# How attention's softmax normaliser is turned into its reciprocal: Ln and Exp by ScalarE in place of a round trip through memory with VectorE's reciprocal

## The chip, the cores and the metric

The kernel runs on one core of a Trainium2 chip, in one launch. Its time is what one execution takes on the device, in microseconds (us). Five engines work side by side, each in its own program order: PE (TensorE, matmuls; PEld is its weight load), DVE (VectorE), ACT (ScalarE), POOL (GpSimd) and SP (SyncE, which here only issues DMAs). POOL and ACT issue DMAs too, in the order of their own instructions.

## The reference

A trunk of two layers on x of 1024 positions by 1024 channels, in fp32. Layer 0 mixes by a gated short convolution, layer 1 by dilated attention; a SwiGLU feed-forward follows each, and a norm ends it. What matters here is the attention (16 heads of 64):

```python
BRANCHES = ((128, 1), (512, 4), (2048, 16))       # window, dilation
...
bias = rel_bias[t5_bucket(jnp.clip(rel, 0) * dilation)]
s = s + bias...; s = jnp.where(mask, s, NEG_INF)
lse = jax.nn.logsumexp(s, axis=-1)
p = jnp.exp(s - lse[..., None])
o = einsum(p, v)                                  # one o and lse for each branch
...
alpha = jax.nn.softmax(jnp.stack(lses, axis=0), axis=0)
o = jnp.sum(alpha[..., None] * jnp.stack(outs, axis=0), axis=0)
return o.reshape(bsz, seq, D_MODEL) @ w_out
```

Weighting the branches by a softmax of their log-denominators is the same as one softmax over the keys of all three: the sum of exp(s) times v over the sum z of exp(s). So a query and head need one 1/z.

## The kernel before, in words

**Layout.** Activations lie with 128 channels on the partitions and 1024 positions along a row; such a [128, 1024] fp32 tile is a page, and 41 pages are handed out in rotation. The 8 banks of PSUM (`bank()`, 128x512 fp32) rotate too: a matmul into a bank waits until the engine that reads the bank's earlier content is done with it. An fp32 product is three matmuls over a high and a low part of each operand; `split` makes them, the high part by ACT (L142) and the low part by DVE (L143). The instructions are issued in the order of the code (`tc.manual_schedule()`), so what is written between two steps of one engine stands between them on the chip.

**Order of the program.** Layer 0 and its feed-forward come first; within it, from 942 us, `bias_tables` makes the tables of the relative bias, with an Exp (L529) and a Ln (L530) on a tile of 16x64. The attention follows, up to about 1470 us, then its feed-forward.

**The attention's loop.** `slot(n, ...)` runs for n = 0 to 16. Slot n computes the scores of head n and the product with the values (P·V) of head n−1, and between these it draws on a list of dense work: value tiles (L1512 to L1517), projections of q and k (L370 to L372, taken out by `emit`, L1138 to L1147) and the output product (L370 to L372, added to x by L492).

- `scores`: PE multiplies into banks (L1569, L1570); DVE reads each bank, adding the bias (L1580, L1589, L1606, L1611), and keeps a running maximum m (L1594 to L1620); POOL spreads the maximum over all partitions into mb (L1623, `partition_all_reduce`).
- `softmax`, in the second half of the slot: five times, DVE subtracts mb (L1631), and ACT takes the Exp in place (L1632).
- `values`, in slot n+1: PE multiplies the exponentials with v into two banks (L1642). v carries 64 columns of ones, so that half of each bank's partitions hold z, 64 times over. ACT copies z (L1665) and o (L1666) out.
- `finish(p)`, once both heads of a pair of heads p are done: 1/z. Its code is a generator whose steps are drawn at fixed places of the slots (the calls on `ending` and `extra`). POOL issues all its DMAs: two of the equal rows of z go to memory (zdram, L1674); come back as zc, 128 partitions by 16 (L1677); DVE takes the reciprocal (L1679); POOL writes it to memory (rdram, L1680) and reads it back spread over 64 partitions, twice, into z (L1683). Up to slot 14 the first four steps fall in an odd slot (two in the first half, one each later) and the end in the next even slot's first half.
- `attended()`: DVE multiplies o by z (L1730), POOL writes the pair to odram (L1731).
- The last pair is written apart: its first half takes DVE's reciprocals straight on the wide tile (L1704, twice 128x256), its second half goes through memory (L1691 to L1721).

`LAG` is 13: up to slot 13 the P·V runs in the slot's second half, after that in its first. From slot 12 on, written pairs are loaded again (tile oin), split, and multiplied by w_out.

Of the kernel before, what the change touches and what calls it, by code (L numbers as in the profile page):

```python
# [13 lines left out]
ALU = mybir.AluOpType  # L14
# [17 lines left out]
WARM = 10  # L32

# [65 lines left out]
def trunk(ctx: ExitStack, tc: tile.TileContext, x, gains_in, cwi, ck, cwo, wqkv, wo, relb,  # L99
# [397 lines left out]
    def bias_tables():  # L497
# [30 lines left out]
        nc.vector.tensor_tensor(out=d, in0=d, in1=m, op=ALU.subtract)  # L528
        nc.scalar.activation(d, d, AF.Exp)  # L529
# [940 lines left out]
    zdram = [[dram.tile([2, S], F32, name=f"{x}dram{n}") for x in "zr"] for n in range(NPAIR)]  # L1470

# [3 lines left out]
    def attention(norm, qk):  # L1475
# [159 lines left out]
        def values(p, a, st):  # L1635
# [27 lines left out]
            for ih in range(2):  # L1663
                s = slice(ih * HALF, (ih + 1) * HALF)
                nc.scalar.activation(z[n0, s], acc[ih][z0], AF.Copy)  # L1665
                nc.scalar.activation(o[n0, s], acc[ih][n0], AF.Copy)  # L1666
            yield

        def finish(p):

            o, z = OZ.pop(p)
            if p < NPAIR - 1:
                zd, rd = zdram[p]
                nc.gpsimd.dma_start(zd, z[0:65:64])  # L1674
                yield
                zc = scope["pool"].tile([128, 16], F32, name="zc", tag="zc", bufs=2)
                nc.gpsimd.dma_start(zc, bass.AP(zd.tensor, zd.offset, [[16, 128], [1, 16]]))  # L1677
                yield
                nc.vector.reciprocal(zc, zc)  # L1679
                nc.gpsimd.dma_start(bass.AP(rd.tensor, rd.offset, [[16, 128], [1, 16]]), zc)  # L1680
                yield
                for a in range(2):
                    nc.gpsimd.dma_start(z[64 * a:64 * a + 64], bass.AP(rd.tensor, rd.offset + a * S, [[0, 64], [1, S]]))  # L1683
                yield
                put_off.append((p, o, z))
                return

            zd, rd = zdram[p]
            wide = lambda t: bass.AP(t.tensor, t.offset, [[HALF, 2], [1, HALF]])
            thin = lambda t: bass.AP(t.tensor, t.offset, [[8, 128], [1, 8]])  # L1690
            nc.gpsimd.dma_start(wide(zd), z[0:65:64, HALF:])  # L1691
            zc = scope["pool"].tile([128, 8], F32, name="zl", tag="zl", bufs=1)
            nc.gpsimd.dma_start(zc, thin(zd))
            acts[p] = page("o_hi", F32R), page("o_lo", F32R)

            def scaled(c0, c1):
                q = slice(c0, c1)
                nc.vector.tensor_tensor(out=o[:, q], in0=o[:, q], in1=z[:, q], op=ALU.mult)
# [4 lines left out]
            for c in (0, 256):  # L1703
                nc.vector.reciprocal(z[:, c:c + 256], z[:, c:c + 256])  # L1704
                scaled(c, c + 256)
                if c:
                    parts(0)
                    nc.scalar.activation(scratch, eps, AF.Sqrt)
                yield

            def rest():
                scaled(HALF, S)
                parts(1)

            last_part.append(rest)
            yield
            ensure(ahead_ao + KT - AO_WIDE)
            nc.vector.reciprocal(zc, zc)
            nc.gpsimd.dma_start(thin(rd), zc)
            for a in range(2):  # L1720
                nc.gpsimd.dma_start(z[64 * a:64 * a + 64, HALF:],  # L1721
                                    bass.AP(rd.tensor, rd.offset + a * HALF, [[0, 64], [1, HALF]]))
# [13 lines left out]
        def slot(n, dense, ndense, late=0, hook=iter(())):  # L1736
# [30 lines left out]
            if lagged:  # L1767
                for i in range(8):
# [4 lines left out]
                    if a and ending and i in (0, 3):  # L1773
                        next(ending[-1])
                    if a == 0 and ending and i == 2:
                        run(ending.pop())
                run(sc)
            else:
# [3 lines left out]
                for i in range(8):  # L1782
# [6 lines left out]
                    if ending and i == 2:  # L1789
                        run(ending.pop())  # L1790
# [7 lines left out]
            for i in range(8):  # L1798
# [4 lines left out]
                if lagged and a and ending and i == 6:  # L1803
                    next(ending[-1])
# [35 lines left out]
        X[:] = [None] * KT  # L1840
        bias = {0: load_bias(0)}
# [236 lines left out]
```

## Time and profile before

| What | Value |
|---|---|
| Time, median of 3 runs | 2137.89 us (2135.56 to 2138.65) |
| Time of the profiled execution | 2136.81 us |
| Its span in the profile | 2135.0 us |
| Mean granted clock of TensorE | 0.996 |
| Stretches at half clock | 3.41 us from 1304.79, 6.83 us from 1355.99, the end from 2127.40 |
| z evictions, L1665, 64x512 | 32, 592 ns each |
| zc reciprocals, L1679, 128x16 | 7, 246 ns each |
| o*z, L1730, 128x1024 | 7, 1217 ns each |
| Waits of POOL, 1110 to 1440 us | zc on zdram 27.1 us in 6; rdram on zc 21.4 us in 5; z on rdram 16.7 us in 4 |

The time of an execution is a little more than its span, which runs from the first to the last instruction that the profiler shows. A row of a timeline gives start and duration in us, engine, line, operation, out<-in, and in brackets the idle time of the engine before it with the event that ended it. A row of waits gives the engine and line that waited, what for, the total, the number and the longest. L and a number is a line of the kernel before.

### The profile page before, as it was taken

The page shows a single profiled execution, that of the slowest core. Times are in us where ns is not written, and L with a number is a line of the kernel's source. Part 1 is how long each engine was busy: PE and PEld are TensorE (multiplying, and loading weights), DVE is VectorE, ACT ScalarE, POOL GpSimd, SP SyncE. Part 2 cuts the span into 40 slices and gives each one's busy share as a digit, 9 for nine tenths or more (in the row PEclk, how much of TensorE's full clock was granted, in tenths as well). Part 3 has the DMA queues.
Part 4 walks back from the last instruction along what each step waited for, and adds up shares of the span by engine and source line. Part 5 has one row for each costly group of instructions (what it writes and reads, how often), then busy time and mean ns, then how long its engine had stood idle before and what let it go on. Part 6 is the DMA issues. An engine that isn't in the chain of part 4 may idle for free. (4 is left out here: it accounts for less than half of the span.)

```text
span 2135.0 us, 31015 instructions
## 1 busy us (share of the span) xinstructions
PE 2103.4 (99%) x11082; PEld 1805.6 (85%) x11082; DVE 1744.7 (82%) x3273; ACT 1009.2 (47%) x1853; POOL 256.5 (12%) x375
## 2 busy tenths in 40 slices
PE   9999999999999999999999999999999999999998
PEld 7788888888888888877899998888788888888887
DVE  8898769988888888868967687777998888888876
ACT  7333426443444554446545544545543434456435
POOL 1000000110101000010322333221011101001000
PEclk9999999999999999999999999999999999999999
DMA  7322642333332576340767777765123333368432
GB/s 219 94 94 70 227 137 71 104 104 104 114 109 99 170 218 197 112 167 30 265 204 182 186 194 216 214 198 160 59 94 105 103 109 113 101 199 240 157 94 79
DMA packets 143449, 304.90 MB, mean 143 GB/s; under 512 B 48972, under 2 KB 55422, under 8 KB 143296
## 3 DMA queue, kind: packets, MB, share of 16 engines
q1 hardware_dynamic: 107488, 201.94, 31.5%
q0 software_dynamic: 28176, 86.29, 12.7%
q10 hardware_dynamic: 7632, 14.70, 1.8%
q8 instruction: 88, 1.44, 0.3%
q14 instruction: 65, 0.53, 0.1%
HBM read 212.48 MB, written 83.05 MB: 138 GB/s over the span
## 5 line engine op out<-in xcount | busy, mean ns | idle before, releaser
L572 PE MATMUL bank<-b,w 128*128 128x512 f32 x1952 | 760.9, 390 | 4.9 <-DVE w L143 4.7
L570 PE MATMUL bank<-b,w 128*128 128x512 f32 x1952 | 762.8, 391 | 2.5 <-ACT w L142 1.7
L571 PE MATMUL bank<-b,w 128*128 128x512 f32 x1952 | 760.4, 390 | 0.6 <-DVE b L881 0.6
L572 PEld LDWEIGHTS bank<-b,w 128*128 128x128 f32 x1952 | 366.4, 188 | 85.8 <-DVE w L143 9.6
L570 PEld LDWEIGHTS bank<-b,w 128*128 128x128 f32 x1952 | 366.7, 188 | 79.5 <-ACT w L142 2.8
L571 PEld LDWEIGHTS bank<-b,w 128*128 128x128 f32 x1952 | 366.7, 188 | 76.0 <-DVE b L881 1.2
L142 ACT ACTIVATE w<-combo 128x512 fp32r<-128x512 f32 (+2 forms) x488 | 249.1, 540 | 231.5 <-DVE combo L190 214.6
L143 DVE TENSOR_TENSOR w<-combo,w 128x512 fp32r<-128x512 f32 (+2 forms) x488 | 276.2, 579 | 37.8 <-ACT w L142 37.1
L576 ACT ACTIVATE part<-bank 128x512 f32<-128x512 f32 x186 | 110.8, 596 | 388.8 <-PE bank L572 385.3
L143 DVE TENSOR_TENSOR w<-raw,w 128x512 fp32r<-128x512 f32 (+2 forms) x342 | 189.6, 575 | 38.6 <-ACT w L142 38.6
L580 DVE TENSOR_TENSOR part<-part,bank 128x256 f32<-128x256 f32 (+1 forms) x366 | 170.5, 495 | 31.2 <-PE bank L572 16.7
L142 ACT ACTIVATE w<-raw 128x512 fp32r<-128x512 f32 (+2 forms) x342 | 166.7, 530 | 44.9 <-PE bank L572 12.2
L370 PE MATMUL bank<-w_hi,w 128*128 128x512 f32 (+1 forms) x400 | 153.3, 383 | 5.1 <-ACT w_hi L142 3.7
L371 PE MATMUL bank<-w_lo,w 128*128 128x512 f32 (+1 forms) x400 | 149.7, 374 | 1.2 <-DVE w_lo L143 1.2
L372 PE MATMUL bank<-w_hi,w 128*128 128x512 f32 (+1 forms) x400 | 149.7, 374 | 0.7 <-DVE w L143 0.7
L800 DVE TENSOR_TENSOR x<-x,bank 128x512 f32<-128x512 f32 x136 | 92.6, 681 | 29.2 <-PE bank L572 29.0
L492 DVE TENSOR_TENSOR x<-x,bank 128x512 f32<-128x512 f32 (+1 forms) x104 | 66.1, 641 | 56.6 <-PE bank L372 56.1
L190 DVE TENSOR_TENSOR combo<-raw 128x512 f32<-128x512 f32 (+1 forms) x172 | 111.1, 646 | 0.0
L370 PEld LDWEIGHTS bank<-w_hi,w 128*128 128x128 f32 x400 | 75.8, 189 | 18.5 <-ACT w_hi L142 3.9
L371 PEld LDWEIGHTS bank<-w_lo,w 128*128 128x128 f32 x400 | 75.7, 189 | 14.9 <-DVE w_lo L143 2.0
L372 PEld LDWEIGHTS bank<-w_hi,w 128*128 128x128 f32 x400 | 75.6, 189 | 14.8 <-DVE w L143 1.6
L563 DVE TENSOR_TENSOR b<-hin,b 128x512 fp32r<-128x512 f32 x126 | 79.5, 684 | 9.4 <-ACT b L562 9.4
(252 smaller groups left out, 3488.6 us busy)
## 6 DMA issues: line engine op xcount, KB each, us to landing
hin<-part SPq DMA_DIRECT2D x126, 256.0 KB
raw<-in_ffn_w_gate SPq DMA_DIRECT2D x44, 512.0 KB
raw<-in_ffn_w_up SPq DMA_DIRECT2D x44, 512.0 KB
part<-sum POOLq DMA_DIRECT2D x72, 256.0 KB, 2.3
raw<-in_ffn_w_down SPq DMA_DIRECT2D x48, 384.0 KB
raw<-in_attn_w_qkv SPq DMA_DIRECT2D x27, 512.0 KB
raw<-in_conv_w_in SPq DMA_DIRECT2D x24, 512.0 KB
part<-part POOLq DMA_DIRECT2D x36, 256.0 KB, 2.4
```

What stands on the lines that cost most here:

```text
L142: nc.scalar.activation(hi, src, AF.Copy)
L143: eng.tensor_tensor(out=lo, in0=src, in1=hi, op=ALU.subtract)
L190: eng.tensor_tensor(out=c, in0=a, in1=b, op=op)
L370: nc.tensor.matmul(b, whi[:, a], ahi[:, s], start=first, stop=False)
L371: nc.tensor.matmul(b, whi[:, a], alo[:, s], start=False, stop=False)
L372: nc.tensor.matmul(b, wlo[:, a], ahi[:, s], start=False, stop=last)
L570: nc.tensor.matmul(b, hi[:, a], bhi, start=start and k == 0, stop=False, skip_group_check=True)
L571: nc.tensor.matmul(b, hi[:, a], blo, start=False, stop=False, skip_group_check=True)
L572: nc.tensor.matmul(b, lo[:, a], bhi, start=False, stop=k == n - 1, skip_group_check=True)
L576: nc.scalar.activation(t, b, AF.Copy)
L580: nc.vector.tensor_tensor(out=t, in0=t, in1=b, op=ALU.add)
L800: nc.vector.tensor_tensor(out=X[n][:, half(h)], in0=X[n][:, half(h)], in1=b, op=ALU.add)
```

## The change

z leaves its banks through Ln in place of Copy, and `finish` is one Exp with scale −1 on the tile of 128x1024, so that z becomes exp(−ln z) = 1/z. The two buffers in memory, zc and the DMAs are gone. `finish` then has a single step, which runs in the first half of the odd slot (and in slot 14), and its pair is ready for `attended()` at the end of that same slot, where it had been the next even slot's. For the last pair, ACT does Exp on one half, DVE multiplies it and it is split, then the other half. Two calls name the activation table set that holds both Exp and Ln, one before the bias tables' Exp, one at the start of the attention.

```diff
@@ -30,6 +30,7 @@
 WINOGRAD = (1, 2, 6, 5, 7, 3, 4)
 DEEP, DEEPER = (2, 4), 10
 WARM = 10
+LN_EXP = "natural_log_exp_and_others"
 
 
 def paired(pairs, chunk, tiles):
@@ -526,6 +527,7 @@
         nc.vector.tensor_tensor(out=m, in0=b2, in1=b3, op=ALU.max)
         nc.vector.tensor_tensor(out=d, in0=b2, in1=b3, op=ALU.min)
         nc.vector.tensor_tensor(out=d, in0=d, in1=m, op=ALU.subtract)
+        nc.scalar.preload_act_table_set(LN_EXP)
         nc.scalar.activation(d, d, AF.Exp)
         nc.scalar.activation(d, d, AF.Ln, bias=1.0)
         nc.vector.tensor_tensor(out=b2, in0=m, in1=d, op=ALU.add)
@@ -1467,8 +1469,6 @@
 
     vdram = [dram.tile([S, 256], F32, name=f"vdram{g}") for g in range(NPAIR // 2)]
 
-    zdram = [[dram.tile([2, S], F32, name=f"{x}dram{n}") for x in "zr"] for n in range(NPAIR)]
-
     def blk(j):
         return (j // 4) * HALF + (j % 4) * 8
 
@@ -1662,7 +1662,7 @@
             z0 = slice(64 - 64 * a, 128 - 64 * a)
             for ih in range(2):
                 s = slice(ih * HALF, (ih + 1) * HALF)
-                nc.scalar.activation(z[n0, s], acc[ih][z0], AF.Copy)
+                nc.scalar.activation(z[n0, s], acc[ih][z0], AF.Ln)
                 nc.scalar.activation(o[n0, s], acc[ih][n0], AF.Copy)
             yield
 
@@ -1670,56 +1670,33 @@
 
             o, z = OZ.pop(p)
             if p < NPAIR - 1:
-                zd, rd = zdram[p]
-                nc.gpsimd.dma_start(zd, z[0:65:64])
-                yield
-                zc = scope["pool"].tile([128, 16], F32, name="zc", tag="zc", bufs=2)
-                nc.gpsimd.dma_start(zc, bass.AP(zd.tensor, zd.offset, [[16, 128], [1, 16]]))
-                yield
-                nc.vector.reciprocal(zc, zc)
-                nc.gpsimd.dma_start(bass.AP(rd.tensor, rd.offset, [[16, 128], [1, 16]]), zc)
-                yield
-                for a in range(2):
-                    nc.gpsimd.dma_start(z[64 * a:64 * a + 64], bass.AP(rd.tensor, rd.offset + a * S, [[0, 64], [1, S]]))
-                yield
+                nc.scalar.activation(z, z, AF.Exp, scale=-1.0)
                 put_off.append((p, o, z))
                 return
-
-            zd, rd = zdram[p]
-            wide = lambda t: bass.AP(t.tensor, t.offset, [[HALF, 2], [1, HALF]])
-            thin = lambda t: bass.AP(t.tensor, t.offset, [[8, 128], [1, 8]])
-            nc.gpsimd.dma_start(wide(zd), z[0:65:64, HALF:])
-            zc = scope["pool"].tile([128, 8], F32, name="zl", tag="zl", bufs=1)
-            nc.gpsimd.dma_start(zc, thin(zd))
+                yield
+
             acts[p] = page("o_hi", F32R), page("o_lo", F32R)
 
-            def scaled(c0, c1):
-                q = slice(c0, c1)
-                nc.vector.tensor_tensor(out=o[:, q], in0=o[:, q], in1=z[:, q], op=ALU.mult)
+            def scaled(h):
+                nc.vector.tensor_tensor(out=o[:, half(h)], in0=o[:, half(h)], in1=z[:, half(h)], op=ALU.mult)
 
             def parts(h):
                 split(o[:, half(h)], [t[:, half(h)] for t in acts[p]])
 
-            for c in (0, 256):
-                nc.vector.reciprocal(z[:, c:c + 256], z[:, c:c + 256])
-                scaled(c, c + 256)
-                if c:
-                    parts(0)
-                    nc.scalar.activation(scratch, eps, AF.Sqrt)
-                yield
-
             def rest():
-                scaled(HALF, S)
                 parts(1)
 
+            nc.scalar.activation(z[:, half(0)], z[:, half(0)], AF.Exp, scale=-1.0)
+            scaled(0)
+            parts(0)
+            yield
+            nc.scalar.activation(z[:, half(1)], z[:, half(1)], AF.Exp, scale=-1.0)
+            scaled(1)
+            nc.scalar.activation(scratch, eps, AF.Sqrt)
+            yield
             last_part.append(rest)
             yield
             ensure(ahead_ao + KT - AO_WIDE)
-            nc.vector.reciprocal(zc, zc)
-            nc.gpsimd.dma_start(thin(rd), zc)
-            for a in range(2):
-                nc.gpsimd.dma_start(z[64 * a:64 * a + 64, HALF:],
-                                    bass.AP(rd.tensor, rd.offset + a * HALF, [[0, 64], [1, HALF]]))
             ensure(ahead_ao + KT - AO_WIDE + 4)
             yield
 
@@ -1770,9 +1747,7 @@
                     if n or i % 2:
                         other(1)
                         used += 1
-                    if a and ending and i in (0, 3):
-                        next(ending[-1])
-                    if a == 0 and ending and i == 2:
+                    if a and ending and i == 0:
                         run(ending.pop())
                 run(sc)
             else:
@@ -1786,8 +1761,6 @@
                     if i >= late and i % 2 == 0:
                         other(1)
                         used += 1
-                    if ending and i == 2:
-                        run(ending.pop())
                 run(sc)
                 run(pv)
                 if a == 0:
@@ -1800,8 +1773,6 @@
                 next(pv, None)
                 if i == (2 if n > LAG + 1 else 5):
                     attended()
-                if lagged and a and ending and i == 6:
-                    next(ending[-1])
                 if not lagged and (i < FIN0 or i > SOFT):
                     next(extra, None)
                 if i in (1, 2):
@@ -1838,6 +1809,7 @@
                     add_to_x(n, {c: b})
 
         X[:] = [None] * KT
+        nc.scalar.preload_act_table_set(LN_EXP)
         bias = {0: load_bias(0)}
         load_kq(0)
         run(value_tiles(0, 0))
```

On ACT, in the bias tables (the tile d of 16x64, between a weight tile's splits), the order before:

```order
L529 ACT_TABLE_LOAD
L529 ACTIVATE d<-d 16x64
L530 ACT_TABLE_LOAD
L530 ACTIVATE d<-d 16x64
L142 ACTIVATE w<-raw 128x512
L880 ACTIVATE b<-x,gains 128x512
```

and now, where the split of `w` is L143:

```order
L530 ACT_TABLE_LOAD
L531 ACTIVATE d<-d 16x64
L532 ACTIVATE d<-d 16x64
L143 ACTIVATE w<-raw 128x512
L882 ACTIVATE b<-x,gains 128x512
```

The Ln has no table load of its own any more, and the split behind it moves up by one instruction.

On POOL, from slot 8 into slot 10 (kq is the projected q and k on its way to memory, odram a finished pair, mb the maximum of a slot), before:

```order
L1731 DMA odram_87<-o 128x1024
L1144 DMA kq_1_2951<-kq_hi 128x512
L1147 DMA kq_1_2951<-kq_lo 128x512
L1674 DMA zdram_103<-z 2x1024
L1677 DMA zc<-zdram_103 128x16
L1623 ISA mb<-m 128x1024
L1144 DMA kq_0_2950<-kq_hi 128x512
L1147 DMA kq_0_2950<-kq_lo 128x512
L1680 DMA rdram_104<-zc 128x16
L1144 DMA kq_0_2950<-kq_hi 128x512
L1147 DMA kq_0_2950<-kq_lo 128x512
L1683 DMA z<-rdram_104 64x1024 x2
```

and now:

```order
L1146 DMA kq_1_2935<-kq_hi 128x512
L1149 DMA kq_1_2935<-kq_lo 128x512
L1623 ISA mb<-m 128x1024
L1146 DMA kq_0_2934<-kq_hi 128x512
L1149 DMA kq_0_2934<-kq_lo 128x512
L1708 DMA odram_88<-o 128x1024
L1146 DMA kq_0_2934<-kq_hi 128x512
L1149 DMA kq_0_2934<-kq_lo 128x512
L1623 ISA mb<-m 128x1024 x2
```

The DMAs of z, zc and rdram are gone from between the others; mb of slot 9 stands behind the kq DMAs alone, and the write of a pair stands in the odd slot.

On DVE, where slot 14's subtractions end and slot 15 begins (lf is the next head's bias add, x the residual that takes the output product), before:

```order
L1631 TENSOR_TENSOR lp<-lp,mb 128x16x24
L1631 TENSOR_TENSOR lp<-lp,mb 128x512
L1730 TENSOR_TENSOR o<-o,z 128x1024
L1679 RECIPROCAL zc<-zc 128x16
L492 TENSOR_TENSOR x<-x,bank 128x512 x2
L143 TENSOR_TENSOR w<-raw,w 128x512
L1580 TENSOR_TENSOR lf<-bank,bias 128x4x64 x4
```

and now, with o*z as L1707, L493 for L492 and L144 for L143:

```order
L1631 TENSOR_TENSOR lp<-lp,mb 128x16x24
L1631 TENSOR_TENSOR lp<-lp,mb 128x512
L1707 TENSOR_TENSOR o<-o,z 128x1024
L493 TENSOR_TENSOR x<-x,bank 128x512 x2
L144 TENSOR_TENSOR w<-raw,w 128x512
L1580 TENSOR_TENSOR lf<-bank,bias 128x4x64 x4
```

The reciprocal that stood ahead of the bank evictions L492 is gone. The order of PE and of SP is the same as before.

## The prediction

> **What bounds the kernel now.** I read the page first, for the engines' shares.
>
> ```profile
> span 2135.0 us, 31015 instructions
> PE 2103.4 (99%) x11082; PEld 1805.6 (85%) x11082; DVE 1744.7 (82%) x3273; ACT 1009.2 (47%) x1853; POOL 256.5 (12%) x375
> ```
>
> TensorE (PE) is busy for 2103.4 of 2135.0 us, and no matmul is edited, so the change can only win what PE waits for, and what its clock loses. Next come the waits of PE (columns: us in total, times, longest) and windows over the attention (columns: us, busy time of PE, PEld, DVE, ACT, POOL, then PE's granted clock, DMA share, GB/s).
>
> ```profile
> PE bank L572 <- DVE w L143: 4.7, 6, 1.7
> PE bank L1569 <- ACT o L1666: 3.8, 3, 2.1
> PE bank L370 <- ACT w_hi L142: 3.7, 1, 3.7
> 1135.00:1440.00 305.00, 293.65 (x2130) 274.67 (x2129) 228.09 (x403) 152.91 (x221) 91.55 (x94) 0.98 0.72 197
> 1160.00:1170.00 10.00, 8.26 (x68) 7.86 (x67) 8.33 (x16) 6.78 (x12) 4.19 (x6) 1.00 0.78 215
> 1300.00:1310.00 10.00, 7.95 (x54) 7.74 (x54) 9.46 (x22) 7.28 (x12) 2.65 (x5) 0.83 0.31 91
> 1350.00:1360.00 10.00, 5.82 (x38) 4.93 (x37) 6.63 (x8) 7.11 (x10) 1.41 (x1) 0.80 0.56 162
> 1360.00:1370.00 10.00, 9.24 (x49) 7.90 (x49) 7.20 (x12) 5.64 (x8) 3.89 (x7) 0.86 0.50 145
> 1440.00:1470.00 30.00, 30.00 (x134) 24.82 (x134) 21.94 (x34) 12.82 (x22) 3.99 (x6) 1.00 0.54 174
> ```
>
> The slots that the change rewrites lie in 1135 to 1440 us. PE idles there for 305.00 − 293.65 = 11.35 us. The clock lost more: 0.83 over 10 us is 1.7 us of lost work, which at half clock is 3.4 us of time; 0.80 and 0.86 are another 2.0 + 1.4 = 3.4 us lost. So some 16.5 us is the most that the slots can give, and only if every gap there goes. I then looked at each gap in the timeline, for what its releaser had itself waited for.
>
> **The change part by part.** The first edit is far from attention, in the bias tables. The rows give start, duration, engine, line, and in brackets the idle time and its releaser.
>
> ```profile
> 944.10 1.28 ACT L530 ACT_TABLE_LOAD   x1
> 945.39 0.26 ACT L530 ACTIVATE d<-d 16x64 f32<-16x64 f32 x1
> 945.55 0.61 ACT L142 ACTIVATE w<-raw 128x512 fp32r<-128x512 f32 x1
> 944.49 0.39 PE L372 MATMUL bank<-w_hi,w 128*128 128x512 f32 x1
> 946.22 0.50 PE L370 MATMUL bank<-w_hi,w 128*128 128x512 f32 x1 [1.34 <-ACT w L142]
> ```
>
> The Ln is preceded by a table load of its own, and the split behind it is what PE waits 1.34 us for. With one set for Exp and Ln the load goes, the split runs 1.28 earlier, and the gap shrinks by as much. **−1.28.** The Trainium skill, "ScalarE: Activation LUTs", section "Table sets: the hidden batching unit", puts a switch at 1283 ns of load and about 1380 ns of drain, about 2.66 us in all. The load agrees, while here the Ln starts 1.29 us after the load does, with no drain to be seen; by the page's 2.66 the whole gap of 1.34 would go, and the term would be −1.34.
>
> Now the odd slots. The round trip's second DMA, zc from zdram, stands in POOL's queue ahead of the partition_all_reduce (mb) on which the softmax hangs. These rows are slots 7 and 9, then slot 12, where POOL had nothing ahead.
>
> ```profile
> 1250.32 0.69 DVE L1620 TENSOR_TENSOR m<-m,lp 128x512 f32<-128x512 f32 x1
> 1252.05 0.54 POOL L1677 DMA_DIRECT2D zc<-zdram  x1 [4.57 <-issue]
> 1252.62 3.18 POOL L1623 PARTITION_ALL_REDUCE mb<-m  x1
> 1286.41 1.13 PE L1642 MATMUL bank<-lf,vx 128*128 128x128 f32 x8 [1.10 <-issue]
> 1293.24 0.69 DVE L1620 TENSOR_TENSOR m<-m,lp 128x512 f32<-128x512 f32 x1
> 1294.47 0.57 POOL L1677 DMA_DIRECT2D zc<-zdram  x1 [6.18 <-DMA zdram<-z]
> 1295.08 3.18 POOL L1623 PARTITION_ALL_REDUCE mb<-m  x1
> 1298.29 1.22 DVE L1631 TENSOR_TENSOR lf<-lf,mb 128x1024 f32<-128x1024 f32 x1 [0.82 <-POOL mb L1623]
> 1304.43 0.38 PE L1569 MATMUL bank<-qa,ka 128*128 128x256 f32 x1 [2.05 <-ACT o L1666]
> 1347.31 0.69 DVE L1620 TENSOR_TENSOR m<-m,lp 128x512 f32<-128x512 f32 x1
> 1348.19 3.22 POOL L1623 PARTITION_ALL_REDUCE mb<-m  x1 [0.52 <-DVE m L1620]
> 1357.42 0.79 PE L370 MATMUL bank<-w_hi,w 128*128 128x512 f32 x1 [3.71 <-ACT w_hi L142]
> ```
>
> In slot 12, mb starts 0.19 us after m ends. In slot 9, m ends at 1293.93 and mb starts at 1295.08, held by a DMA that waited 6.18 us for the z it reads back. Without it mb comes 1.15 − 0.19, about 1.0 earlier. DVE had idled only 0.82 before the subtraction, so the subtraction, the five Exps and the evictions of z and o behind them come 0.8 earlier; PE's gap of 2.05 ends with the second o and becomes 1.25. **−0.8**, between 0 and −1.0. That gap is also what dropped the clock (0.83 above). A stretch of 3.4 us at half clock costs 1.7; with a gap of 1.25 I expect none, since the gap of 1.24 at 1167.96 (below) left the clock at 1.00 in its window. **−1.7**, between 0 and −1.7. The Trainium skill, "TensorE: Matmul & The Clock Gate", section "What's actually happening", drops the clock after at least one idle window of about 3.4 us, and lets the windows run free. Here a gap of 2.05 was enough, so the measurement decides; by the page's threshold this term would not hang on the gap at all, and the sum would be 1.7 smaller.
>
> In slot 7, m ended at 1251.01 and mb was 1.6 late in the same way. No PE gap follows in that slot; the next is 1.10 at 1286.41 in slot 8, put down to issue; by the order of the eight banks it is a wait for one that DVE empties. DVE's o*z (1.22, below) leaves the even slot and enters the odd one. Between 0 and −1.10, I take **−0.3**, near zero because a whole slot lies between.
>
> The gap of 3.71 at 1357.42 is the split of the loaded attention behind the Exps of slot 12. POOL was not late there, so I leave it, **0**, with −1.7 as the far end should the slot before run earlier. In slots 11 and 13 the added Exp stands ahead of evictions on ACT; I give back **+0.2**, between 0 and 6 × 1.06 (second rival).
>
> Slot 15 is the last place:
>
> ```profile
> 1410.38 0.25 DVE L1679 RECIPROCAL zc<-zc 128x16 f32<-128x16 f32 x1 [5.12 <-DMA zc<-zdram]
> 1411.23 0.38 PE L1569 MATMUL bank<-qa,ka 128*128 128x256 f32 x1 [0.33 <-DVE x L492]
> 1419.96 0.69 DVE L1620 TENSOR_TENSOR m<-m,lp 128x512 f32<-128x512 f32 x1
> 1420.57 1.22 DVE L1730 TENSOR_TENSOR o<-o,z 128x1024 f32<-128x1024 f32 x1
> 1427.28 1.16 PE L1642 MATMUL bank<-lf,vx 128*128 128x128 f32 x8 [1.01 <-ACT lf L1632]
> ```
>
> DVE stands for 5.12 us at the reciprocal, waiting for the round trip's data, and behind it in order are the bank evictions (x, L492) that PE waits 0.33 for, and the maxima that lead to the Exp that PE waits 1.01 for. The reciprocal, its wait, and the o*z at 1420.57 in that slot all go; DVE then waits for PE instead. Both gaps close: **−1.34**, between 0 and −1.34.
>
> What is added lies on ACT, at these prices, with its room:
>
> ```profile
> L1632 ACT ACTIVATE lf<-lf x16: 1057/1060/1066, 1126.3 to 1426.2; 128x1024 f32<-128x1024 f32 x16
> L1632 ACT ACTIVATE lh<-lh x16: 612/616/618, 1127.3 to 1427.1; 128x512 f32<-128x512 f32 x16
> ACT lf L1632 <- DVE lf L1631: 92.0, 16, 14.3
> 1439.10 1.74 DVE L1704 RECIPROCAL z<-z 128x256 f32<-128x256 f32 x1
> 1167.96 0.38 PE L1569 MATMUL bank<-qa,ka 128*128 128x256 f32 x1 [1.24 <-ACT o L1666]
> 1169.16 0.84 ACT L1517 ACTIVATE v<-bank,r 128x256 f32<-128x256 f32 x2
> 1172.38 0.83 PE L1642 MATMUL bank<-lf,vx 128*128 128x128 f32 x6
> ```
>
> Seven Exps of 128x1024 at 1.06 and two of 128x512 at 0.62 are 8.7 us, where ACT idles 92.0 us ahead of the softmax's Exps, 5.75 a slot. An eviction with Ln in place of Copy is one pass of ACT over the same 64x512 either way, and I price it at 0; were it dearer, it would eat of the same 92.0 first. The last pair loses two reciprocals of 1.74 on DVE, but PE is busy 30.00 of 30.00 us from 1440 to 1470, so that is **0**. The load that stood ahead of the first softmax Exp stands ahead of the first value tile; it precedes an eviction that can't begin before PE has filled the bank: 0, at worst +1.28.
>
> The sum is −1.28 − 0.8 − 1.7 − 0.3 + 0.2 − 1.34 = −5.2. The profiled execution took 2136.81 us (1.8 more than its span), which gives 2131.6. The median of the three runs is 2137.89, 1.1 above the profiled one, so the forecast is **2132.7**, its own range 2130 to 2135.
>
> **The rivals.** First, *given back later*: DVE's o*z moves into the ends of odd slots, behind the subtractions, and evictions of lf for the next slot queue there; slots 7 to 9 end as late as before, and only the tables' load and part of slot 15 are left, −1.28 − 0.7: 2135.9. For it: DVE is 9.46 of 10 us busy at 1300 to 1310. Against: one o*z a pair as before, and a reciprocal and its waits fewer. Chance 0.20.
>
> Second, *slower*: ACT works in order, and the Exp (1.06) stands ahead of the v or kq_hi evictions in the first half of six odd slots. In slot 5 the second v eviction ends at 1170.01 and its bank is used again at 1172.38, a slack of 2.37; the rival decides if the Exp, with the kca or weight split queued ahead of it, delays such an eviction by more than that. Then up to 6 × 1.06 = 6.4 of new gaps, and one half-clock stretch of 1.7, stand against −1.28 − 1.34: +5.5, 2143.4. Against it is the slack, twice one Exp. Chance 0.14.
>
> Third, *a larger gain*: the slots before 1357 run earlier, so that part of the 3.71 goes (−1.7) and one of the two half-clock stretches behind it (−1.7): 2129.3. Against: nothing removed stands ahead of that mb. Chance 0.14.
>
> Fourth, *the clock drops elsewhere*: the 1.24 at 1167.96 or the new 1.25 falls so that a stretch is still lost: +1.7, 2134.4. For it: 2.05 was enough, 1.24 was not, and nothing here shows what lies between. Chance 0.06. The free-running windows of the Trainium skill's rule above would give this time too.
>
> Fifth, *it doesn't do what it says*: Ln and Exp load tables in turn. Seven pairs at two loads of 1.28 are 18 us on ACT, some of it on the path: 2145 or more. The order of after shows no load between them. The same page of the Trainium skill says that the set natural_log_exp_and_others holds both functions. Chance 0.02.
>
> **How the numbers follow.** The forecast has the remaining 0.44. A measurement of this kernel tells about 0.2%, 4.3 us, from no change, so faster means under 2133.6. The forecast gives 0.36 of its 0.44 to faster and 0.08 to the same; the larger gain 0.14 to faster; the given-back case 0.02, 0.16 and 0.02; the clock 0.01 and 0.05; the second and fifth 0.16 to slower. Faster 0.53, same 0.29, slower 0.18. The range is 2128 (the larger gain, with 1.3 for runs that differ) to 2140 (the slower rival at half its gaps); it leaves out the rest of that rival and the fifth, and some of the tails.
>
> **What would show it.** Right: PE's gap at the bias tables near 0.1; no zc wait on POOL, mb within 0.3 us of m in slots 7 and 9; the gap near 1304 at about 1.25 with clock 1.00 in its window; no gaps in slot 15; the 3.71 still there. Wrong: PE waiting at L1512 or L370 for v or kq_hi, table loads beside L1673, or new gaps under DVE's evictions after an odd slot's o*z.

## The result, and the profile after

| | before | after |
|---|---|---|
| Median of 6 runs each | 2138.27 us (2135.56 to 2139.18) | 2129.78 us (2129.60 to 2131.69) |
| Ratio | | 0.9962, 95% interval 0.9952 to 0.9972 |
| Profiled execution | 2136.81 us, span 2135.0 | 2129.80 us, span 2128.0 |

The changed kernel is faster by 8.5 us in the medians, 7.0 us between the two profiled executions; 2132.7 was forecast, with a range of its own of 2130 to 2135 that the median misses by 0.2, inside the wide range of 2128 to 2140. First the page of after: ACT has 6.5 us more to do, DVE 4.9 and POOL 22.1 less.

```profile
span 2128.0 us, 30922 instructions
PE 2102.3 (99%) x11082; PEld 1806.5 (85%) x11082; DVE 1739.8 (82%) x3262; ACT 1015.7 (48%) x1861; POOL 234.4 (11%) x335
```

The timeline of after at the places that the prediction showed: ACT and PE at the bias tables; DVE's last maximum (L1620), POOL's mb (L1623) and PE in slots 7 to 9; the gap of slot 12; PE in slot 15.

```profile
943.61 0.26 ACT L531 ACTIVATE d<-d 16x64 f32<-16x64 f32 x1 [0.46 <-DVE d L529]
943.90 0.26 ACT L532 ACTIVATE d<-d 16x64 f32<-16x64 f32 x1
944.07 0.61 ACT L143 ACTIVATE w<-raw 128x512 fp32r<-128x512 f32 x1
944.28 0.39 PE L373 MATMUL bank<-w_hi,w 128*128 128x512 f32 x1
944.73 0.50 PE L371 MATMUL bank<-w_hi,w 128*128 128x512 f32 x1
1247.82 0.69 DVE L1620 TENSOR_TENSOR m<-m,lp 128x512 f32<-128x512 f32 x1
1248.68 3.22 POOL L1623 PARTITION_ALL_REDUCE mb<-m  x1 [3.71 <-DVE m L1620]
1283.74 0.38 PE L1642 MATMUL bank<-lf,vx 128*128 128x128 f32 x2
1290.39 0.69 DVE L1620 TENSOR_TENSOR m<-m,lp 128x512 f32<-128x512 f32 x1
1291.29 3.21 POOL L1623 PARTITION_ALL_REDUCE mb<-m  x1 [6.39 <-DVE m L1620]
1300.67 0.39 PE L1569 MATMUL bank<-qa,ka 128*128 128x256 f32 x1 [1.14 <-ACT o L1666]
1352.24 0.79 PE L371 MATMUL bank<-w_hi,w 128*128 128x512 f32 x1 [3.72 <-ACT w_hi L143]
1405.60 0.28 PE L1569 MATMUL bank<-qa,ka 128*128 128x256 f32 x1
1420.37 1.05 PE L1642 MATMUL bank<-lf,vx 128*128 128x128 f32 x8
```

The Ln follows the Exp with no load between, and PE's gap of 1.34 is 0.06 (944.28 + 0.39 to 944.73). mb starts 0.17 and 0.21 us after m ends, where it was 1.61 and 1.15. The gap of 1.10 is gone, that of 2.05 is 1.14, and the two of slot 15 are gone. The 3.7 of slot 12 stands. The windows of after (same columns as before) show the clock at 1.00 where it was 0.83, and the other half-clock stretch unchanged in kind.

```profile
1135.00:1440.00 305.00, 296.95 (x2147) 277.93 (x2146) 231.18 (x404) 166.08 (x240) 71.24 (x58) 0.99 0.68 189
1300.00:1310.00 10.00, 9.32 (x80) 9.33 (x81) 8.49 (x20) 4.84 (x8) 2.85 (x4) 1.00 0.64 184
```

Both programs issue the same matmuls in the same order, so the two traces can be laid side by side matmul by matmul. The table gives how much earlier PE is in after at the end of each stage, and the step that the stage adds.

| Stage | PE earlier by | step | forecast |
|---|---|---|---|
| up to the bias tables (944) | 0.21 | −0.21 | 0 |
| bias tables | 1.49 | −1.28 | −1.28 |
| up to the end of slot 8 | 1.40 | +0.09 | 0 |
| the gap at 1286 | 2.74 | −1.34 | −0.3 |
| the gap at 1304 | 3.76 | −0.92 (and −0.10 ahead of it) | −0.8 |
| half clock behind it | 5.24 | −1.48 | −1.7 |
| slots 10 to 14, with the 3.7 | 5.15 | +0.09 | +0.2 |
| slot 15 | 7.01 | −1.86 | −1.34 |
| the rest | 7.27 | −0.26 | 0 |

The first row is the start of the program, which no edit touches. The span is 7.0 shorter, since what follows the last matmul differs by 0.3. A gap that closes wins some 0.25 more than the idle time in its bracket (1.10 gives 1.34; 0.33 and 1.01 give 0.59 and 1.27), because matmuls that wait for nothing overlap: eight of L1642 take 1.05 together at 1420.37, where one lasts 0.28 on average.

### The profile page after: what moved, and what is told of

The parts are those of the page before. It is cut to its first block, busy times and chain, and to the rows that moved or that the text cites. A ratio compares the mean times of both kernels' runs of the same rounds, so it can differ in the third digit from the quotient of the medians.

```text
span 2128.0 us, 30922 instructions
## 1 busy us (share of the span) xinstructions
PE 2102.3 (99%) x11082; PEld 1806.5 (85%) x11082; DVE 1739.8 (82%) x3262; ACT 1015.7 (48%) x1861; POOL 234.4 (11%) x335
## 4 chain that ended last, share of the span: by engine, by line
PE 85%; DVE 7%; ACT 3%; DMA 2%; issue 2%; POOL 1%; SPq 0%; DVEq 0%; ACTq 0%; POOLq 0%
PE bank L574 19%; PE bank L572 19%; PE bank L573 19%; PE bank L373 4%; PE bank L372 4%; PE bank L371 4%; PE bank L664 3%; PE bank L667 3%; PE bank L666 3%; PE bank L1642 2%; POOL mb L1623 1%; PE bank L1512 1%; PE bank L1513 1%; PE bank L1514 1%; DVE w L144 1%
## 5 line engine op out<-in xcount | busy, mean ns | idle before, releaser
L143 ACT ACTIVATE w<-combo 128x512 fp32r<-128x512 f32 (+2 forms) x488 | 249.1, 540 | 230.2 <-DVE combo L191 213.3
L144 DVE TENSOR_TENSOR w<-combo,w 128x512 fp32r<-128x512 f32 (+2 forms) x488 | 277.7, 583 | 37.6 <-ACT w L143 36.9
L144 DVE TENSOR_TENSOR w<-raw,w 128x512 fp32r<-128x512 f32 (+2 forms) x342 | 189.5, 576 | 37.5 <-ACT w L143 37.5
L143 ACT ACTIVATE w<-raw 128x512 fp32r<-128x512 f32 (+2 forms) x342 | 166.9, 530 | 44.4 <-PE bank L574 11.5
L493 DVE TENSOR_TENSOR x<-x,bank 128x512 f32<-128x512 f32 (+1 forms) x104 | 66.4, 644 | 62.6 <-PE bank L373 61.4
```

The costliest lines, as they stand in the source:

```text
L143: nc.scalar.activation(hi, src, AF.Copy)
L144: eng.tensor_tensor(out=lo, in0=src, in1=hi, op=ALU.subtract)
```

## The experiments

The theory: time was won where the round trip had stood in the way on its queues, POOL's (slots 7 to 9) and DVE's (slot 15), besides the tables' load. The rivals: VectorE's relief, the new place of o*z, or any way without the round trip would have done. The times of before in each comparison were taken beside the run, on the same chip. The changed kernel was not run beside them, so differences from its 2129.78 are good to about 1 us: the medians of before range from 2138.12 to 2139.04.

**One table load.** The kernel before, and:

```diff
+        nc.scalar.preload_act_table_set("natural_log_exp_and_others")
         nc.scalar.activation(d, d, AF.Exp)
         nc.scalar.activation(d, d, AF.Ln, bias=1.0)
```

> The kernel before with one edit: the set that holds Exp and Ln is named ahead of the bias tables' Exp. If the switch of tables is all that PE waits for there, the gap of 1.34 us near 946 us shrinks to about 0.1, nothing else moves, and the time is 2138.3 - 1.3 = 2137.0. The rival, that another wait takes its place (the high part of the next weight tile, or its low part by VectorE), leaves the gap over 0.8 and the time within 0.5 of before.

Measured: 2136.47 against 2139.04, ratio 0.9992 (0.9983 to 1.0001): too little for the runs to tell, but the timeline shows it: PE's matmul follows within 0.06, and PE runs 1.3 earlier from there, up to a gap of 1.25 at 1242 that before does not have. The third row is slot 9, unedited here:

```profile
944.35 0.39 PE L372 MATMUL bank<-w_hi,w 128*128 128x512 f32 x1
944.80 0.50 PE L370 MATMUL bank<-w_hi,w 128*128 128x512 f32 x1
1304.51 0.38 PE L1570 MATMUL bank<-qa,ka 128*128 128x256 f32 x1 [3.51 <-ACT o L1667]
```

The gap that was 2.05 in the profile of before is 3.51 with the same code, and no half clock follows it, where the 2.05 was followed by a loss of 1.48. What the round trip costs, and in which form, varies from one execution to the next, and one profile of before is one draw of it.

**The round trip put back, unused.** The changed kernel, and for pairs 0 to 5 (shortened; the steps are drawn at or near their old places again):

```diff
                 nc.scalar.activation(z, z, AF.Exp, scale=-1.0)
                 put_off.append((p, o, z))
+                if p == NPAIR - 2: return
+                nc.gpsimd.dma_start(zd, o[0:65:64]);  yield
+                nc.gpsimd.dma_start(zc, <zd as 128x16>);  yield
+                nc.gpsimd.dma_start(<rd as 128x16>, zc);  yield
```

> The changed kernel with the first three DMAs of the round trip put back on POOL at their old places for pairs 0 to 5, reading rows of o, their result used by nothing (the last read, the reciprocal, and pairs 6 and 7 stay out). Theory one, POOL's queue: mb starts 1.0 to 1.6 late again in slots 7 and 9, the gaps near 1284 and 1300 come back (1.1 and about 2.0), perhaps with the half-clock stretch: +2.4 to +4.1 on 2129.8, so 2132.2 to 2133.9. Theory two, VectorE (the reciprocal gone, o*z elsewhere) is what paid in these slots: no more than +0.4, 2130.2.

Measured: 2135.24, that is 5.5 over the changed kernel and above both forecasts. PE's rows in slots 8, 9 and 12, POOL's in slot 11:

```profile
1286.36 0.35 PE L1644 MATMUL bank<-lf,vx 128*128 128x128 f32 x1 [0.48 <-PE bank L373]
1303.49 0.38 PE L1571 MATMUL bank<-qa,ka 128*128 128x256 f32 x1 [1.16 <-ACT o L1668]
1330.92 0.56 POOL L1683 DMA_DIRECT2D zc<-zdram  x1 [7.41 <-DMA oin<-odram]
1331.52 3.18 POOL L1625 PARTITION_ALL_REDUCE mb<-m  x1
1359.11 0.79 PE L371 MATMUL bank<-w_hi,w 128*128 128x512 f32 x1 [6.12 <-ACT w_hi L143]
```

Theory one, but in other places than before: in slots 7 and 9 mb starts 0.17 and 0.20 behind m, so the delay expected there did not return. Slot 5 has a small one, 0.84, and the gap in slot 8 is back at half its size. The large one is in slot 11: mb is held there, 4.42 behind m, by a read that waited 7.41 us beside the loads of oin, and PE's 3.7 in slot 12 becomes 6.1. This profile is of the slowest of the ten runs; of the 6.9 us by which PE ends later than in after, 1.9 fall ahead of 100 us, where no edit reaches, and 4.9 between 1280 and 1360. Theory two allowed 0.4. So a read that POOL must wait for, ahead of mb, costs here without any work of VectorE. That the other transfers decide which slot pays is likely, but not shown.

**The read moved behind mb.** The kernel before, and:

```diff
-                    if a and ending and i in (0, 3):
+                    if a and ending and i == 0:
                         next(ending[-1])
...
                 run(sc)
+                if a and ending:
+                    next(ending[-1])
```

> The kernel before, all its arithmetic kept, with POOL's read of zc moved behind the slot's partition_all_reduce in the odd slots. Theory one: slots 8 and 9 gain as in the changed kernel, 1.3 + 1.1 and perhaps 1.5 of clock, while the tables and slot 15 stay as they were: 2138.3 - 2.4 to - 3.9, so 2134.4 to 2135.9. Theory two: 2138.3 within 1, since the delay is VectorE's. A third way: the later zc holds VectorE at the reciprocal, which stands ahead of the next slot's bank evictions, and the time is 2139 to 2142.

Measured: 2138.60 against 2139.04, ratio 0.9996 (0.9987 to 1.0006): the same. The trace shows why. PE in slot 9 and slot 12, DVE between them:

```profile
1303.20 0.38 PE L1569 MATMUL bank<-qa,ka 128*128 128x256 f32 x1 [1.06 <-ACT o L1666]
1340.36 0.25 DVE L1679 RECIPROCAL zc<-zc 128x16 f32<-128x16 f32 x1 [3.37 <-DMA zc<-zdram]
1358.27 0.80 PE L370 MATMUL bank<-w_hi,w 128*128 128x512 f32 x1 [7.27 <-ACT w_hi L142]
```

Up to slot 9 it wins what the change wins: mb follows m in 0.10, the gap at 1286 is gone, that of 2.05 is 1.06 with no half clock; by PE's matmuls 3.9 us between 1266 and 1308. Then the later zc holds DVE (14.3 us in 5 waits, 5.1 in one before), which delays slot 12's maxima, and the 3.71 becomes 7.27: 3.6 are given back there, and 1.0 more goes in slot 15. This is the expectation's third way, behind theory one's gain. POOL's wait was the loss in slots 7 to 9, as theory one has it, but moving it along one queue handed it to the next.

**VectorE's reciprocal in place.** The changed kernel, z leaving by Copy, and (the same on the two halves of the last pair):

```diff
-                nc.scalar.activation(z, z, AF.Exp, scale=-1.0)
+                nc.vector.reciprocal(z, z)
```

> The changed kernel with Copy on z's way out and VectorE's reciprocal on the whole 128x1024 in place of ScalarE's Exp (in the last pair on the two halves): the round trip is gone, but ScalarE is not used. By 1.74 us for 128x256 a reciprocal is 7 us, ahead of VectorE's bank evictions in the first half of the odd slots, where it idles some 2.5 a slot. Theory: VectorE is on the path there, +4.5 for each of 7 pairs, 2160, at most 7 x 7 = 49 more. The rival, that the round trip's waits alone were the cost and any engine will do: under 2135.

Measured: 2168.28, 38.5 over the changed kernel. The groups and the waits of PE:

```profile
L1673 DVE RECIPROCAL z<-z 128x1024 f32<-128x1024 f32 x7 | 45.8, 6549 | 6.3 <-ACT z L1665 6.3
PE bank L1642 <- DVE lf L1580: 13.1, 4, 6.6
```

Seven reciprocals of 6.55 us are 45.8, and most of it reaches the end, part of it as lost clock: 27.3 us at half clock between 1216 and 1391, where after has 6.83. The round trip had bought this: on 128x16 the same values take 0.25. So leaving out the round trip was not enough by itself; VectorE had no room for the wide reciprocal.

**Two more passes of ScalarE.** The changed kernel, and behind each Exp of 128x1024:

```diff
+                for _ in range(2):
+                    nc.scalar.activation(z, z, AF.Copy)
```

> The changed kernel with two more passes of ScalarE (Copy of z onto itself, 128x1024) behind each of the seven Exps: 3 x 1.06 in place of 1.06, to find how much room stands where the Exp was put. Theory: ScalarE idles 5 us a slot, but evictions in the odd slots' first half wait behind it, and the banks' slack is about 2.4; gaps of 0.3 to 2.1 grow in two to four odd slots: +1 to +6, 2131 to 2136. The rival, room enough: within 0.5 of 2129.8. More than +10 would say that the Exp itself already fills its place.

Measured: 2139.06, 9.3 over the changed kernel, more than expected. PE's new gaps, the first of which after had at 0.33:

```profile
1172.95 0.58 PE L1569 MATMUL bank<-qa,ka 128*128 128x256 f32 x1 [1.69 <-ACT v L1517]
1213.23 0.38 PE L1569 MATMUL bank<-qa,ka 128*128 128x256 f32 x1 [1.97 <-ACT v L1517]
1333.34 0.38 PE L1642 MATMUL bank<-lf,vx 128*128 128x128 f32 x1 [0.78 <-ACT v L1517]
```

The first two also dropped the clock, for 6.83 and 3.41 us. So ScalarE's 92 us of idle time was not room at this place: what follows the Exp in its order are evictions, and one Exp nearly fills their slack.

**The table set not named.** The changed kernel without its two lines `preload_act_table_set(LN_EXP)`.

> The changed kernel without the two lines that name the table set. In its order, Exp and Ln then load their tables in turn: 36 more loads in the attention, 1.28 us each, one of them in every slot between the softmax's five Exps and the Ln on z's way out of the banks. Theory: this one is on the path where PE waits for those evictions (slots 3, 9) and eats the slack elsewhere, so +1.28 in 5 to 15 slots: 2136 to 2149. The rival: ScalarE idles over 5 us a slot and hides them, under +2: 2130 to 2132; then naming the set was not needed.

Measured: 2150.62, 20.8 over the changed kernel and 12.5 over before (ratio to before 1.0059, 1.0044 to 1.0074). ACT's loads, and PE in slot 3:

```profile
L1664 ACT ACT_TABLE_LOAD x15 | 19.2, 1283 | 0.2
L1631 ACT ACT_TABLE_LOAD x8 | 10.3, 1283 | 8.1 <-DVE lf L1630 8.0
L1672 ACT ACT_TABLE_LOAD x7 | 9.0, 1283 | 0.1
1170.65 0.58 PE L1568 MATMUL bank<-qa,ka 128*128 128x256 f32 x1 [3.53 <-ACT o L1665]
```

It is 40 loads against 9 (the expectation, with 36 more, miscounted, and so did the prediction, with 18 us): 31 × 1.28 = 40 us on ACT, of which half reaches the end, part of it as lost clock (23.9 us at half clock in the attention, 6.83 in after). The prediction's fifth rival, tables in turn, is real and would have made the change slower; naming the set is what avoids it. The Trainium skill, "ScalarE: Activation LUTs", section "Table sets: the hidden batching unit", asks for work in the order of sets for this reason, and the trace agrees; its single load for Ln and Exp held here only where the set was named.

**Pair 6 alone through memory.** The changed kernel with the old `finish` for p == NPAIR − 2 and Copy for its z.

> The changed kernel with pair 6 alone sent through memory and VectorE's 128x16 reciprocal as before (its z leaves the banks by Copy). Theory: VectorE stands about 5 us at that reciprocal in slot 15 again and PE's gaps there (0.3 and 1.0, or 1.7 by the shift of the two traces) come back: 2131.1 to 2131.5, and nothing else moves. The rival: slot 15 gained because the slots before it ran earlier, and it stays within 0.3 of 2129.8.

Measured: 2132.77 (2131.24 to 2134.76). The timeline of slot 15:

```profile
1405.52 0.25 DVE L1681 RECIPROCAL zc<-zc 128x16 f32<-128x16 f32 x1 [6.23 <-DMA zc<-zdram]
1406.37 0.38 PE L1571 MATMUL bank<-qa,ka 128*128 128x256 f32 x1 [0.31 <-DVE x L493]
1422.41 0.38 PE L1644 MATMUL bank<-lf,vx 128*128 128x128 f32 x1 [1.01 <-ACT lf L1634]
```

Both gaps are back, 1.8 us by PE's matmuls, so slot 15's gain is pair 6's round trip and nothing earlier. The median moved by 3.0, over the 1.3 to 1.7 expected; the profiled execution, 2131.91, by 2.1. What the other runs lost beyond that, no profile shows.

**o*z in the even slots again.** The changed kernel, and:

```diff
-                    attended()
+                    if not (lagged and a): attended()
```

> The changed kernel, with o*z and the write of a pair put back into the next even slot (1/z is made by ScalarE in the odd slot as in the change). If only the round trip paid, nothing moves: 2129.8 within 0.5. If its place paid too, o*z (1.22) stands ahead of VectorE's eviction of kq in slot 8 again, and part of the 1.1 near 1284 comes back: +0.3 to +1.2, 2130.1 to 2131.0. If the given-back rival of the prediction was right on VectorE at the odd slots' ends, it is faster by up to 1.

Measured: 2129.74 against the changed kernel's 2129.78. The place of o*z is worth nothing that shows: from 1180 us to the end, PE's distance to after changes by 0.1. That also speaks against the prediction's first rival, which the median had ended already. Its windows show one thing more:

```profile
1164.00:1171.30 7.30, 5.75 (x34) 5.34 (x33) 6.52 (x18) 7.19 (x12) 0.00 (x0) 0.77 0.68 182
1280.00:1290.00 10.00, 9.99 (x67) 8.99 (x66) 8.40 (x17) 4.93 (x6) 1.09 (x2) 1.00 1.08 290
```

PE is busy for 9.99 of 10.00 us where the gap of 1.10 was, so that gap did not hang on o*z ahead of the eviction of kq. And here a half-clock stretch fell near 1168, which the profile of after doesn't have.

**The splits of slot 12, earlier.** The 3.7 that the change left was tried on its own: the changed kernel, with the four splits of oin drawn in the first four steps of slot 12's second half, ahead of the Exps:

```diff
+                if n == LAG - 1:
+                    next(hook, None)
...
-                if i >= SOFT:
+                if i >= SOFT and n != LAG - 1:
                     next(hook, None)
```

> The changed kernel, with the splits of the loaded attention drawn at the first four steps of slot 12's second half in place of the last four: three of them stand ahead of the softmax's subtractions and Exps, in the time in which mb is made. If PE's 3.7 us near 1352 are only the order on ScalarE, the gap falls under 0.5 and the 6.83 us at half clock with it: -3.2 - 3.4, down to 2123.2. The rival: the low parts on VectorE (three at about 1.2 us) outlast mb by some 0.5 to 1.5, slot 12's Exps and slot 13 come late by that, and the time is 2125 to 2128.

Measured: 2124.43, 5.3 under the changed kernel, ratio to before 0.9934 (0.9919 to 0.9949). The gap and its 6.83 us of half clock are gone; one new gap stands in slot 13, where PE waits for vx, the values with their ones, read back from memory:

```profile
1350.00:1360.00 10.00, 10.00 (x62) 8.87 (x61) 9.72 (x21) 9.38 (x14) 2.17 (x4) 1.00 0.30 79
1362.81 0.35 PE L1642 MATMUL bank<-lf,vx 128*128 128x128 f32 x1 [1.87 <-DMA vx<-vdram]
```

The time lies between the 2123.2 of the theory and the 2125 to 2128 of the rival. The rival's delay is there, but it reaches PE by another way than expected: the low parts on VectorE delay the Exps (lf, the first of them, starts at 1350.35, where after has 1347.51), and behind the Exps on ScalarE stands the eviction of the last value tile, on which the load of vx hangs. Two other places for the splits were tried, first the last four steps of slot 11:

```diff
-            if n == LAG - 1:
+            if n == LAG - 2:
                 done.update(load_attended(range(AO)))
-            hook = halves() if n == LAG - 1 else iter(())
+            hook = halves() if n == LAG - 2 else iter(())
```

> The changed kernel, with the loaded attention fetched one slot earlier and its four splits drawn in slot 11's last four steps, behind that slot's Exps. The 3.7 near 1352 and the half-clock stretch go (-6.6 of 2129.8, 2123.2), and slot 13's gap of 1.87 of the earlier split trial doesn't come; but four low parts at 1.2 to 1.6 us on VectorE stand ahead of slot 12's bank evictions, against a slack of about 2.4: a new gap of 1 to 4 near 1325 to 1330, so 2124 to 2128. The rival, that VectorE has the room there: 2122.5 to 2123.5.

and, with the same earlier load, two splits at steps 4 and 6 of slot 11's second half and two at the first two steps of slot 12's:

> The changed kernel, with two of the splits in slot 11's second half behind its Exps and two in slot 12's, ahead of its subtractions while mb is made (3.2 us on GpSimd, two low parts of 1.6 on VectorE). Theory: the 3.7, the half-clock stretch and the 1.87 of the first split trial all go with at most 0.5 given back: 2122.5 to 2123.7, the fastest of all. The rival: VectorE's two splits at the end of slot 11 delay slot 12's maxima and thereby its Exps, and the gap moves there: 2124 to 2126, no better than the first split trial.

Measured: 2129.71 and 2127.84, so 5.3 and 3.4 over the first place and over every forecast made for them. PE's rows of slots 12 and 13 in the one, of slot 13 in the other:

```profile
1341.85 0.36 PE L1512 MATMUL bank<-w_hi,b 128*128 128x256 f32 x1 [0.97 <-DVE lf L1580]
1366.92 0.35 PE L1642 MATMUL bank<-lf,vx 128*128 128x128 f32 x1 [3.03 <-DMA vx<-vdram]
```

```profile
1365.86 0.42 PE L1642 MATMUL bank<-lf,vx 128*128 128x128 f32 x1 [3.06 <-DMA vx<-vdram]
```

Both make slot 12's Exps later (lf at 1353.94 and 1352.91, where the first place had 1350.35), and with them the value tile's eviction and vx. VectorE did not have the room at slot 11's end: in the one it shows in PE's 0.97, and in the other the gap moved and did not go, as its rival had it, though it cost more.

**The value tile's eviction first.** The first split trial, and:

```diff
-                if i == (3 if lagged else SOFT):
+                if i == (5 if n == LAG - 1 else 3 if lagged else SOFT):
```

> The first split trial (all four splits in slot 12's first four steps), with that slot's softmax drawn two steps later, which on ScalarE alone puts the eviction of the last value tile ahead of the five Exps in place of behind them; the other engines' orders are the same. In the first split trial PE waited 1.87 us in slot 13 for vx, loaded from what this eviction lets GpSimd write. If the eviction's place is the cause, the write starts some 7 us earlier, the 1.87 goes, and the time is 2124.4 - 1.9 = 2122.5. The rival: vx's load waits for another transfer, or the Exps, a step later, hold PE instead, and it stays at 2124 to 2125.

Measured: 2121.63 against before's 2138.70, ratio 0.9922 (0.9909 to 0.9936): 8.2 us under the changed kernel, the fastest of all. Its waits of PE from 1090 to 1500 us, in full:

```profile
PE bank L1569 <- ACT o L1666: 2.7, 3, 1.1
PE bank L1569 <- ACT v L1517: 0.3, 1, 0.3
```

The wait for vx is gone, so the place of that one eviction, behind the Exps, was its cause. (The profile is again of the slowest run, 2123.94.)

## Why the prediction was right, and where its sizes were off

The direction, the wide range and the places of the gains came out: five of the signs that the prediction named for a right step are in the timeline above, and of the gaps that it named for a wrong one only a small one came. The size was off: the gain is 8.5 where 5.2 was forecast. The median lies next to the 2129.3 of the third rival, a larger gain out of the 3.71, but that is chance: the 3.71 stands. By its steps:

- **Tables, −1.28**: −1.28, and alone in the first experiment. No drain appeared: the Ln had started 1.29 after its load did, and PE keeps a gap of 0.06. The Trainium skill, "ScalarE: Activation LUTs", section "What ACT_TABLE_LOAD costs" (the prediction gave the figure under the section that follows it), has 2.66 with a drain, which would have left no gap; the measurement decides. The Ln on z's way out was priced at 0 over Copy, and took the same 592 ns.
- **Slot 9, −0.8, and the clock, −1.7**: −0.92 and −1.48. The mechanism held, but DVE's free 0.82 ahead of the subtraction did not set the size. In after, DVE idles as long there:

```profile
1292.39 1.33 DVE L1148 TENSOR_TENSOR kq_lo<-kq,kq_hi 128x512 fp32r<-128x512 f32 x1 [0.70 <-ACT kq_hi L1145]
1294.54 1.23 DVE L1631 TENSOR_TENSOR lf<-lf,mb 128x1024 f32<-128x1024 f32 x1 [0.82 <-POOL mb L1623]
```

  The row of kq_lo ahead took 2.25 in before and 1.33 now, so VectorE was ready earlier too, and the step is the 0.94 by which mb moved closer to m. The clock's part belongs to these two executions: the first experiment, with the code of before, lost 3.51 there as idle time and nothing as clock.
- **The gap at 1286, −0.3**: −1.34. This is the term that was mis-sized. Its range, 0 to −1.10, held nearly all of it, but the value was taken "near zero because a whole slot lies between". A slot doesn't absorb a delay here. These are the rows of mb in slot 8, where POOL was not late in either kernel, first of before and then of after, and those of slots 7 and 8 in the run with the read moved behind mb:

```profile
1271.49 3.22 POOL L1623 PARTITION_ALL_REDUCE mb<-m  x1 [0.64 <-issue]
```

```profile
1268.63 3.22 POOL L1623 PARTITION_ALL_REDUCE mb<-m  x1 [0.66 <-DVE m L1620]
```

```profile
1252.32 3.22 POOL L1623 PARTITION_ALL_REDUCE mb<-m  x1 [3.63 <-DVE m L1620]
1271.25 3.22 POOL L1623 PARTITION_ALL_REDUCE mb<-m  x1 [0.64 <-issue]
```

  In after, slot 8's mb comes 2.86 earlier while PE is 1.40 earlier, but o*z has changed its slot as well. The moved read leaves o*z where it was: there mb is 1.20 later than before in slot 6 (1233.55 against 1232.35), then 0.30 earlier in slot 7 and 0.24 earlier in slot 8. The 1.5 won on POOL in slot 7 is still 1.4 in slot 8, and the gap at 1286 is closed. The unused round trip shows the reverse, with o*z where after has it: mb of slots 5 to 8 is 2.72, 2.79, 2.80 and 2.80 later than in after while PE is 1.95 later, so that slot 5's 0.8 comes through three slots undiminished, to the gap of 0.48 in slot 8. So POOL's lateness, and not o*z's place, made that gap.
- **Slot 15, −1.34**: −1.86, past the far end of its range, with pair 6 alone answering for 1.8. The step added up the two idle times, 0.33 and 1.01, and left out that each closed gap wins some 0.25 more.
- **Given back, +0.2 in slots 11 and 13**: nothing there; instead slot 3 has a new gap of 0.33 behind a value tile's eviction that the Exp precedes, 0.60 with what follows it. That is the second rival's mechanism at its point of decision (the text put that place in slot 5; by the sixteen mb it is slot 3). The slack of 2.37 was misread: the matmul that waits for this eviction in after (L1569 at 1169.16) is the one that started at 1170.51 in before, 0.50 behind the eviction's end at 1170.01, and not the L1642 at 1172.38. Two more passes carried the loss to +9.3.
- **The 3.71, 0**: 3.72. It was a matter of order on ScalarE in slot 12, as the trials with the splits show.
- **The median 1.1 above the profiled execution**: for before it is 1.5 in six runs, for after 0. Before, all with round trips, spreads over 2135.4 to 2142.5 in the runs of all comparisons; five of after's six lie within 0.4. The first two experiments show how a round trip's waits differ between executions, which fits; that it is all of the spread is not shown.

So of the 2.9 us between forecast and result, 1.0 is the gap at 1286, 0.5 slot 15, 1.1 the allowance on the median; the rest are small steps of both signs.

## What to carry to other kernels

A short DMA that an in-order queue must wait for is priced by what stands behind it, and where slots are chained, a delay is handed on at full size until something idles; moving it along the queue handed it to the next engine here. A function moved to an engine with idle time needs room at its place, not on average: look at the slack of the buffers whose release stands behind it. Two functions of ScalarE in alternation need one named set; here the loads without it cost 20.8 us, where the edit with it wins 8.5.

## What the runs showed of the hardware that was not expected

The granted clock can drop for gaps well under its own stretch. The stretches of the clock record start on a grid of 3.41 us: the two in before, at 1304.79 and 1355.99, lie 51.20 apart, 15 times 3.413. In the trial with o*z in the even slots, two gaps of 1.07 and 0.49 us between two edges of this grid (1164.44 and 1167.85) were followed by 3.41 us at half clock; in after, nearly the same gaps (1.04 and 0.51) fell on both sides of an edge (1166.64), and the clock stayed at 1.00. The run with two splits in each slot also has both gaps in one window, 1.55 in all, and lost the clock; the run with pair 6 alone has 1.47 in one and did not. This is the prediction's fourth rival, and it comes and goes by execution. The Trainium skill, "TensorE: Matmul & The Clock Gate", section "What's actually happening", has the windows run free, which agrees; its threshold of a whole idle window of about 3.4 us does not, and the measurement decides.

No single idle time within a window explains all runs. In before, 1.6 us near 58 left the clock alone, and the 3.51 of slot 9 in the first experiment, cut by an edge at 1302.82 into 1.8 and 1.7, did too. What decides between some 1.5 and 1.8 stays open.
